# One RWKV-7 and FoX encoder block on one core: the correlation operand of a head pair written for both heads by one VectorE instruction each, the second head's half copied to its tile by ScalarE

## The chip, the core and the metric

The kernel runs on one core of one Trainium2 chip. The metric is the device time of one execution in microseconds. A core has five engines with a queue each, which work side by side and wait for one another by semaphores: TensorE (PE in the profile, its weight loads PEld), VectorE (DVE), ScalarE (ACT), GpSimd (POOL) and SyncE (SP, here only the issuing of transfers). Each queue is worked off in order.

## What is computed

One layer on 512 frames of 1024 channels: a half-step SwiGLU block, then two token mixers side by side on one input projection, then a second half-step block and a norm. The part that matters is the RWKV-7 mixer with 8 heads of 64:

```
kk = k * k_k;  kk = kk / max(sqrt(sum(kk * kk)), 1e-12)      # per head
k  = k * (1 + (a - 1) * k_a)
step: sa    = state . a_t                                     # a_t = -kk, b_t = kk * a
      state = state * w_t + sa b_t^T + v_t k_t^T
      y_t   = state . r_t
```

The kernel runs this recurrence over chunks of 32 frames. Within a chunk it needs the products of the "write" rows (kk·a and k, divided by the running decay) with the "read" rows (-kk and r, times the running decay), masked to the lower triangle, and the inverse of a triangular matrix made of them.

## The kernel before

All weights come as float32, and most products are done as three matmuls of a high and a low part (`mm3`, lines 170 to 172). For each block of 128 columns of the input projection there is a load (L155, SyncE), a high part by ScalarE (`whi`, L162), a low part by VectorE (`wlo`, L163), 24 matmuls of 128 by 512 into a PSUM bank (`pk`, `pgt` for a gate, `pv` later for FoX's v), and then one VectorE instruction that scales the result by the norm (`u`, L1223, or `gs`, L1253).

The 8 heads are 4 pairs; a pair lies on 128 partitions, one head in each half. `step(p)`, called for p = 0 to 3, prepares one pair. It runs the columns k, r and v of the pair and one gate. In between:

- k and r are shifted by a frame (ScalarE L1099, then VectorE L1100). ScalarE makes kk and its square, the square is split (`khi`, `klo`, L192 and L193) and summed over each head by two matmuls with a block matrix (`pn`, L1302 and L1303). ScalarE makes the inverse root `krn` in three steps (L1305, L1307, L1308), VectorE multiplies it in (L1309).
- VectorE scans the decays (L1289), ScalarE makes their two exponentials Pi and Pp (L1294, L1295).
- The write operand `BK[p]` holds k (L1297) and kk·a (L1312) for both heads on 128 partitions. The read operand is `G[p][q]`, one tile per head q of [128, 16 chunks, 2, 32]; head q's own half of the partitions takes -kk·Pp (L1315) and r·Pp (L1319).
- TensorE multiplies the two for each chunk and head (`gp`, L1329: 32 matmuls, each in two passes). The result goes, masked by VectorE (L1333, four instructions a pair), to the other half of `G[p][q]`, so that each tile holds operand and products. GpSimd stores the products to memory (Ld, L1341) for the inversion.
- r·k·r_k is summed over each head by two more matmuls (`rk` L1346, `rhi` and `rlo`, L1351 and L1352) for the bonus `bon`, which SyncE stores (L1356).

After the four pairs Ld is read back and VectorE inverts the triangular matrices (L1375, L1377), with weight splits in between. From then on the order of VectorE, ScalarE and TensorE is written out by hand. In `step` it is not: the order in which the instructions of the stage stand in each queue is set by the scheduler from the program's dependencies and its own estimate of times, except where a line ties one instruction behind another (`issue_after`). Thus an edit in `step` can move other instructions too.

Of the kernel before, what the change touches and what calls it, by code (L numbers as in the profile page):

```python
# [13 lines left out]
ALU = mybir.AluOpType  # L14
# [12 lines left out]
C = 32  # L27
# [50 lines left out]
def kernel(  # L78
# [24 lines left out]
    dve, act, pe = [Queued(e, False) for e in (nc.vector, nc.scalar, nc.tensor)]  # L103
# [14 lines left out]
    def bank(name, pool_=None):  # L118
        pool_ = pool_ or pm
        return pool_.tile([P, T], F32, tag="b", name=name)  # L120
# [70 lines left out]
    def split(dst_hi, dst_lo, src, hi_eng="act"):  # L191
        cast = act.copy(dst_hi, src) if hi_eng == "act" else dve.tensor_copy(dst_hi, src)  # L192
        return cast, dve.tensor_tensor(dst_lo, src, dst_hi.bitcast(F32), op=ALU.subtract)  # L193
# [7 lines left out]
    def on(do, *a):  # L201
        return lambda: do(*a)
# [95 lines left out]
    def pc(i):  # L298
        return par[:, i:i + 1]
# [345 lines left out]
    class Wide:  # L645
# [240 lines left out]
        def column(s, ps):  # L886
            s.rc = s.small[4]
            for i in range(2):
                pe.transpose(ps[:, i * P:(i + 1) * P], s.nrm.rstd[:, i * P:(i + 1) * P], ident[:])
            for i in range(2):  # L890
                dve.tensor_copy(s.rc[:, i:i + 1], ps[:, i * P:i * P + 1])
# [145 lines left out]
    op = o1.enter_context(tc.tile_pool(name="o1", bufs=1, side="right"))  # L1037
# [37 lines left out]
    with ExitStack() as mx:  # L1075
# [3 lines left out]
        G = [[sp.tile([P, NC, 2, C], F32, name=f"G{p}{q}", tag=f"G{p}{q}") for q in range(2)] for p in range(NP)]  # L1079
# [126 lines left out]
        ch = lambda t: t[:].rearrange("p (c t) -> p c t", t=C)  # L1206
        alt = {"Pi": Tall[:, 0:T], "kk": Tall[:, T:2 * T], "Pp": Tall[:, 2 * T:2 * T + NC * (C + 1)]}

        def prep(name, p, n=T):
            if p % 2 == 0:  # L1210
                return alt[name]
            t = t2.tile([P, n], F32, name=name, tag=name)
            return t[:]

        def work(name, dt=F32):
            late = name in ("kka", "rk", "bon")
            return t2.tile([P, T], dt, name=name, tag="sb" if late else "sa", bufs=3 if late else 5)
# [40 lines left out]
        def plain_gate(m):  # L1258
            gate = Gate(m)
            gate.go()  # L1260
            gate.out()
            return gate.mms
# [3 lines left out]
        def half(q):  # L1266
            return slice(q * 64, (q + 1) * 64)

        def step(p):
            if p % 3 == 0:  # L1270
                k, r = spare[2], spare[3]
            else:
                k, r = [t2.tile([P, T], F32, name=f"{n}{p}")[:] for n in "kr"]
            v = vs[p]
            cz, a = za[p]
            BK = BKs[p]
            if p:
                column(DA, p, k, 4)
            kk = prep("kk", p)
            act.activation(kk[:], k[:], AF.Copy, scale=pc(PAR_KK + p))  # L1280
            sq = work("ksq")
            act.activation(sq[:], kk[:], AF.Square)
            hi, lo = work("khi", F32R), work("klo", F32R)
            split(hi[:], lo[:], sq[:])
            t = work("kt")
            act.activation(t[:], a[:], AF.Identity, bias=nka[:, p:p + 1], scale=pc(PAR_KA + p))
            dve.scalar_tensor_tensor(k[:], t[:], 1.0, k[:], op0=ALU.add, op1=ALU.mult)
            with tc.issue_after(after[-1].ins) if after else ExitStack():
                dve.tensor_tensor_scan(cz[:], cmask[:], cz[:], initial=0.0, op0=ALU.mult, op1=ALU.add)  # L1289
            Pp = prep("Pp", p, NC * (C + 1)).rearrange("p (c t) -> p c t", t=C + 1)  # L1290
            pool.memset(Pp[:, :, 0:1], 1.0)
            Pi = prep("Pi", p)
            with tc.issue_after(logs.ins):
                act.activation(Pi[:], cz[:], AF.Exp, scale=DEC)  # L1294
                act.activation(Pp[:, :, 1:C + 1], ch(cz), AF.Exp, scale=-DEC)  # L1295
            pool.tensor_copy(PC[:, p, :], Pp[:, :, C])
            after.append(dve.tensor_tensor(BK[:, :, 1, :], ch(k), ch(Pi), op=ALU.mult))  # L1297

            mms = column(0, p, r, 0) if p else spread
            ps = bank("pn", pf)  # L1300
            with tc.issue_after(mms[2].ins):
                pe.matmul(ps[:], bonesr[:], hi[:], start=True, stop=False)  # L1302
                pe.matmul(ps[:], bonesr[:], lo[:], start=False, stop=True)  # L1303
            rn = work("krn")
            act.activation(rn[:], ps[:], AF.Relu, bias=tiny[:, 1:2])  # L1305
            with tc.issue_after(logs.ins):
                act.activation(rn[:], rn[:], AF.Ln, bias=tiny[:, 0:1])  # L1307
            act.activation(rn[:], rn[:], AF.Exp, scale=-0.5)  # L1308
            dve.tensor_tensor(kk[:], kk[:], rn[:], op=ALU.mult)  # L1309
            ka = work("kka")  # L1310
            dve.tensor_tensor(ka[:], kk[:], a[:], op=ALU.mult)
            dve.tensor_tensor(BK[:, :, 0, :], ch(ka), ch(Pi), op=ALU.mult)  # L1312
            for q in range(2):
                s = slice(q * 64, (q + 1) * 64)
                dve.scalar_tensor_tensor(G[p][q][s, :, 0, :], ch(kk)[s], -1.0, Pp[s, :, 0:C],  # L1315
                                         op0=ALU.mult, op1=ALU.mult)
            for q in range(2):
                s = slice(q * 64, (q + 1) * 64)
                dve.tensor_tensor(G[p][q][s, :, 1, :], ch(r)[s], Pp[s, :, 1:C + 1], op=ALU.mult)  # L1319
            column(2 * DA, p, v, 8)  # L1320
            mms = plain_gate(p)


            gps = [pr.tile([P, NC // 2, 2, C], F32, tag="b", name="gp") for _ in range(2)]
            with tc.issue_after(mms[5].ins):
                for c in range(NC):
                    for q in range(2):
                        o = half((q + c + 1) % 2)
                        gm = pe.matmul(gps[q][o, c // 2], BK[half(q), c], G[p][q][half(q), c], start=True, stop=True)  # L1329
            for q in range(2):  # L1330
                for odd in range(2):
                    o = half((q + odd + 1) % 2)
                    dve.tensor_tensor(  # L1333
                        G[p][q][half(1 - q), odd::2].rearrange("p c a t -> p c (a t)"),
                        gps[q][o].rearrange("p c a t -> p c (a t)"),
                        gmask[o].rearrange("p a t -> p (a t)").unsqueeze(1).broadcast_to([64, NC // 2, 2 * C]),
                        op=ALU.mult)
            for q in range(2):
                r0 = (1 - q) * 64
                un = (q * NP + p) * NC  # L1340
                nc.gpsimd.dma_start(Ld[un:un + NC].rearrange("c s t -> s c t"), G[p][q][r0:r0 + C, :, 0, :])  # L1341
                pool.memset(G[p][q][r0:r0 + C, :, 0, :], 0.0)


            rk = work("rk")
            dve.scalar_tensor_tensor(rk[:], r[:], pc(PAR_RK + p), k[:], op0=ALU.mult, op1=ALU.mult)  # L1346
            ps = bank("pn", pr)
            hi, lo = work("rhi", F32R), work("rlo", F32R)
            split(hi[:], lo[:], rk[:])
            with tc.issue_after(gm.ins):  # L1350
                pe.matmul(ps[:], bonesr[:], hi[:], start=True, stop=False)  # L1351
                pe.matmul(ps[:], bonesr[:], lo[:], start=False, stop=True)  # L1352
            bon = work("bon")
            dve.tensor_tensor(bon[:], ps[:], v[:], op=ALU.mult)
            act.activation(bon[:], bon[:], AF.Identity, bias=pc(PAR_LB + p))
            nc.sync.dma_start(bsave[p], bon[:])  # L1356

        for p in range(NP):
            step(p)
# [21 lines left out]
        for i in range(2):  # L1381
            for q in range(2):
                o = i * 64 + q * C
# [61 lines left out]
        for kg, (wh, wl) in enumerate(vw):  # L1445
            for b in range(NB):
                bs = slice(b * P, (b + 1) * P)
                for k in range(2):
                    kk = kg * 2 + k
                    mm3(vps[b][:], mix.hi[kk][:, bs], mix.lo[kk][:, bs], wh[:, k, :], wl[:, k, :],  # L1450
                        kk == 0, kk == KD - 1)
        for b in range(NB):
            o = vtp.tile([P, T], F32, name=f"vt{b}", tag=f"vt{b}")
# [39 lines left out]
        for q in range(2):  # L1493
            o = (1 - q) * 64
# [11 lines left out]
        for q in range(2):  # L1506
            o = (1 - q) * 64
# [9 lines left out]
        for q in range(2):  # L1517
            pool.memset(Rs[0][half(q), :, q, :], 0.0)
            for i in range(RN):
                o = (1 - q) * 64  # L1520
# [6 lines left out]
        op = plan.op  # L1527
        summed, gone = [op("SP", 0.0, None, later=us, frees=frees) for us, frees in ((3.0, ()), (3.5, ["w"]))]
        o = op("ACT", 0.69, b1.log, summed, rank=SCAN, takes=["t"], frees=["pf"])
        o = op("ACT", 0.63, b1.root, o, rank=SCAN)  # L1530
# [197 lines left out]
        for m in range(NP + 3, 2 * KD):  # L1728
            g = Held()
            w, o = columns("pgt", COL_GA + m * P)  # L1730
# [11 lines left out]
            o = op("DVE", 0.61, result, o, rank=NEXT, takes=["gs"], frees=["pm"])  # L1742
            if m + 1 < 2 * KD:
                o = op("ACT", 0.55 if tanhs else 1.84, opened, o, *roots, rank=ROWS)
# [150 lines left out]
        o = []  # L1895
        for p in range(NP):
            o = op("ACT", 0.63, on(part_y, p), *outs[p], *sees, *o, rank=FILL)
            o = [op("DVE", 0.69, on(part_l, p), o, rank=FILL)]
# [292 lines left out]
```

## Time and profile before

| | |
|---|---|
| runs | 1089.47 us median of 3 (1088.84 to 1091.12) |
| profiled execution | 1088.9 us, span 1087.0 us |
| granted TensorE clock, mean | 0.998 |
| `step`, the four pairs | about 367 to 460 us of the span |
| read operand writes, L1315 and L1319 | 16 of 64 by 512, about 0.68 us each |
| mask multiplies, L1333 | 16 of 64 by 512, 0.69 us each |

The page has the busy time of each engine, the span in 40 slices, the chain of work that ended last and the costliest groups of instructions. A row of the timeline has the start, the duration, the engine, the line, the operation, what is written and read, and in brackets the idle time of the engine before it with what ended it. Matmuls overlap: a row of 0.39 us is followed by the next after 0.23 us. A row of the chain has start, duration and what ran.

### The profile page before, as it was taken

What the parts mean: (1) busy time and instruction counts of PE and PEld (TensorE: products, weight loads), DVE (VectorE), ACT (ScalarE), POOL (GpSimd) and SP (SyncE); (2) the same over time, 40 slices, a digit from 0 to 9 for tenths busy, and PEclk for the clock granted to TensorE, in tenths of its full rate; (3) what the DMA queues carried; (4) which work ended last, traced back from release to release, by engine and by line L of the source; (5) the groups of instructions that cost most, each with busy time, mean ns of one, the idle gap of its engine ahead of it and who ended that gap; (6) DMA issues with size and microseconds to landing.
All of it is one profiled execution on the core that took longest, in us unless ns stands there. A gap on an engine that the chain in (4) does not pass through costs nothing.

```text
span 1087.0 us, 16960 instructions
## 1 busy us (share of the span) xinstructions
PE 1076.6 (99%) x6442; PEld 880.3 (81%) x6442; DVE 839.1 (77%) x1163; ACT 669.2 (62%) x1051; POOL 210.7 (19%) x255
## 2 busy tenths in 40 slices
PE   9999999999999999999999999999999999999997
PEld 7888888888887887788777777888888888888886
DVE  7997676789865689878777867867597766699874
ACT  6765556575655755435889776524576555576654
POOL 1221220134203202311000030122311212114210
PEclk9999999999999999999999999999999999999999
DMA  7989888879936334354223244635967978869972
GB/s 222 253 174 235 203 174 205 183 148 189 232 118 179 104 104 117 110 145 125 60 60 94 81 130 145 198 117 191 255 153 177 202 205 185 191 151 202 236 188 78
DMA packets 139726, 177.13 MB, mean 163 GB/s; under 512 B 9726, under 2 KB 75838, under 8 KB 139646
## 3 DMA queue, kind: packets, MB, share of 16 engines
q0 software_dynamic: 33328, 70.40, 34.0%
q1 hardware_dynamic: 105582, 104.21, 31.3%
q10 hardware_dynamic: 736, 1.45, 0.3%
q8 instruction: 51, 0.84, 0.3%
q14 instruction: 29, 0.24, 0.1%
HBM read 163.51 MB, written 12.52 MB: 162 GB/s over the span
## 4 chain that ended last, share of the span: by engine, by line
PE 93%; DVE 5%; ACT 1%; issue 1%; DVEq 0%; ACTq 0%
PE P L98 39%; PE P L172 5%; PE P L171 5%; PE P L170 5%; PE pgt L98 5%; PE spot L98 3%; PE lp L98 3%; PE pq L98 3%; PE ppj L98 2%; PE pb L98 2%; PE pa L98 2%; PE pw L171 1%; PE pw L170 1%; PE pw L172 1%; PE f L98 1%; DVE wlo L163 1%
## 5 line engine op out<-in xcount | busy, mean ns | idle before, releaser
L98 PE MATMUL P<-sraw,q 128*128 128x512 f32 x344 | 91.3, 389 | 0.0
L162 ACT CAST whi<-raw 128x1024 fp32r<-128x1024 f32 (+2 forms) x42 | 40.4, 962 | 59.0 <-issue 19.3
L98 PEld LDWEIGHTS P<-sraw,q 128*128 128x128 f32 x344 | 64.6, 188 | 13.4
L98 PE MATMUL P<-swhi,q 128*128 128x512 f32 x224 | 71.5, 390 | 0.0
L98 PE MATMUL P<-sraw,wxh 128*128 128x512 f32 x200 | 68.4, 394 | 0.0
L163 DVE TENSOR_TENSOR wlo<-raw,whi 128x1024 fp32r<-128x1024 f32 (+2 forms) x43 | 48.3, 1123 | 12.5 <-ACT whi L162 11.3
L98 PE MATMUL P<-swhi,wxh 128*128 128x512 f32 x144 | 57.0, 396 | 0.0
L98 PE MATMUL P<-swhi,wxl 128*128 128x512 f32 x144 | 56.2, 390 | 0.0
L98 PE MATMUL P<-swlo,wxh 128*128 128x512 f32 x144 | 56.1, 390 | 0.0
L688 POOL DMA_DIRECT2D cb<-in_ffn_w_dram x20 | 24.1, 1204 | 150.0 <-DVE cd L98 85.1
L98 PE MATMUL P<-sraw,wxl 128*128 128x512 f32 x136 | 53.0, 390 | 0.0
L688 POOL DMA_DIRECT2D cd<-in_ffn_w_dram x24 | 29.5, 1228 | 103.0 <-DVE swlo L98 38.6
L98 PEld LDWEIGHTS P<-swhi,q 128*128 128x128 f32 x224 | 42.1, 188 | 8.7
L98 ACT COPY RD<-spot 32x128 f32<-32x128 f32 (+2 forms) x128 | 39.8, 311 | 13.8 <-PE spot L98 11.4
L98 PE MATMUL P<-swlo,q 128*128 128x512 f32 x112 | 43.6, 389 | 0.0
L98 PEld LDWEIGHTS P<-sraw,wxh 128*128 128x128 f32 x200 | 37.2, 188 | 7.3
L98 ACT CAST sraw<-cd 128x1024 fp32r<-128x1024 f32 x30 | 31.5, 1051 | 15.0 <-PE P L98 11.5
L98 DVE TENSOR_TENSOR swlo<-ca,swhi 128x1024 fp32r<-128x1024 f32 x24 | 29.2, 1222 | 14.0 <-ACT swhi L98 14.0
L98 DVE TENSOR_TENSOR swlo<-cc,swhi 128x1024 fp32r<-128x1024 f32 x20 | 24.5, 1224 | 19.0 <-ACT swhi L98 18.7
L98 DVE TENSOR_TENSOR u<-P,u 128x512 f32<-128x512 f32 x52 | 34.1, 684 | 5.8 <-ACT u L98 5.8
L170 PE MATMUL pk<-xh,whi 128*128 128x512 f32 x96 | 38.0, 396 | 0.4 <-DVE u L1223 0.4
L547 POOL DMA_DIRECT2D ca<-in_ffn_w_dram x16 | 19.3, 1205 | 96.4 <-DVE swlo L98 66.4
(621 smaller groups left out, 3431.5 us busy)
## 6 DMA issues: line engine op xcount, KB each, us to landing
raw<-in_w_in_dram SPq DMA_DIRECT2D x40, 512.0 KB
cc<-in_ffn_w_dram SPq DMA_DIRECT2D x36, 512.0 KB
cb<-in_ffn_w_dram POOLq DMA_DIRECT2D x36, 512.0 KB, 5.9
cb<-in_ffn_w_dram SPq DMA_DIRECT2D x32, 512.0 KB
cd<-in_ffn_w_dram POOLq DMA_DIRECT2D x32, 512.0 KB, 7.7
ca<-in_ffn_w_dram POOLq DMA_DIRECT2D x32, 512.0 KB, 7.1
ca<-in_ffn_w_dram SPq DMA_DIRECT2D x20, 512.0 KB
cd<-in_ffn_w_dram SPq DMA_DIRECT2D x18, 512.0 KB
```

The lines of the kernel that those rows point to most:

```text
L98: q.last = do(*a, **kw)
L162: (hi_eng or act).copy(hi[:], raw[:])
L163: (eng or dve).tensor_tensor(lo[:], raw[:], hi[:].bitcast(F32), op=ALU.subtract)
L170: pe.matmul(ps, whi, xhi, start=first, stop=False, skip_group_check=onto)
L171: pe.matmul(ps, whi, xlo, start=False, stop=False, skip_group_check=onto)
L172: return pe.matmul(ps, wlo, xhi, start=False, stop=last, skip_group_check=onto)
L547: nc.gpsimd.dma_start(s.sum[g], src, accum_op=ALU.add)
L688: nc.gpsimd.dma_start(to, s.block(b, n, h), accum_op=ALU.add)
```

## The change

The r and kk parts of the read operand are written for both heads at once, into the first head's tile, by one VectorE instruction each over 128 partitions. ScalarE then copies the second head's half of that tile into the same place of the second head's tile. TensorE's correlation reads both heads' operand from the first tile. The lines behind it have moved up by four: L1329 is L1325, the masks L1333 are L1329, L1351 is L1347 and so on.

```diff
-            for q in range(2):
-                s = slice(q * 64, (q + 1) * 64)
-                dve.scalar_tensor_tensor(G[p][q][s, :, 0, :], ch(kk)[s], -1.0, Pp[s, :, 0:C],
-                                         op0=ALU.mult, op1=ALU.mult)
-            for q in range(2):
-                s = slice(q * 64, (q + 1) * 64)
-                dve.tensor_tensor(G[p][q][s, :, 1, :], ch(r)[s], Pp[s, :, 1:C + 1], op=ALU.mult)
+            dve.scalar_tensor_tensor(G[p][0][:, :, 0, :], ch(kk), -1.0, Pp[:, :, 0:C], op0=ALU.mult, op1=ALU.mult)
+            dve.tensor_tensor(G[p][0][:, :, 1, :], ch(r), Pp[:, :, 1:C + 1], op=ALU.mult)
+            act.copy(G[p][1][half(1)], G[p][0][half(1)])
             column(2 * DA, p, v, 8)
             mms = plain_gate(p)
...
-                        gm = pe.matmul(gps[q][o, c // 2], BK[half(q), c], G[p][q][half(q), c], start=True, stop=True)
+                        gm = pe.matmul(gps[q][o, c // 2], BK[half(q), c], G[p][0][half(q), c], start=True, stop=True)
```

Since the scheduler sets the order, all three engines' queues change in this stage. On TensorE, the rows around the correlation of pair 1 (`G_2540` and `G_2541` are the pair's two tiles, `pn` the head sums, `pk` a column, `pgt` gate 2), before:

```order
L1329 MATMUL gp<-G_2541,BK_2547 64x64
L1351 MATMUL pn<-rhi,bonesr 128x512
L1352 MATMUL pn<-rlo,bonesr 128x512
L1302 MATMUL pn<-khi,bonesr 128x512
L1303 MATMUL pn<-klo,bonesr 128x512
L172 MATMUL pgt<-xh_2584,wlo 128x512
```

and after:

```order
L170 MATMUL pk<-xh_2584,whi 128x512
L171 MATMUL pk<-xl_2585,whi 128x512
L1325 MATMUL gp<-G_2540,BK_2547 64x64 x32
L1347 MATMUL pn<-rhi,bonesr 128x512
L1348 MATMUL pn<-rlo,bonesr 128x512
L172 MATMUL pk<-xh_2584,wlo 128x512
```

The block stood two matmuls into gate 2; it now stands two matmuls into the v column of pair 2, which is 24 matmuls earlier, and the sums of pair 2's squares (`khi`, `klo`) have left it: they come 17 matmuls further on, and 14 apart.

Again on TensorE, the rows from the correlation of pair 2 (`G_2542` and `G_2543`) to the first sum of pair 3's squares, before:

```order
L1329 MATMUL gp<-G_2543,BK_2548 64x64
L1351 MATMUL pn<-rhi,bonesr 128x512
L1352 MATMUL pn<-rlo,bonesr 128x512
L170 MATMUL pk<-xh_2584,whi 128x512
L171 MATMUL pk<-xl_2585,whi 128x512
L172 MATMUL pk<-xh_2584,wlo 128x512
L1302 MATMUL pn<-khi,bonesr 128x512
```

and after:

```order
L1325 MATMUL gp<-G_2542,BK_2548 64x64 x32
L1347 MATMUL pn<-rhi,bonesr 128x512
L1348 MATMUL pn<-rlo,bonesr 128x512
L171 MATMUL pk<-xl_2445,whi 128x512
L172 MATMUL pk<-xh_2444,wlo 128x512
L170 MATMUL pk<-xh_2478,whi 128x512
L171 MATMUL pk<-xl_2479,whi 128x512
L172 MATMUL pk<-xh_2478,wlo 128x512
L170 MATMUL pk<-xh_2478,whi 128x512
L171 MATMUL pk<-xl_2479,whi 128x512
L172 MATMUL pk<-xh_2478,wlo 128x512
L1302 MATMUL pn<-khi,bonesr 128x512
```

The correlation stood at the end of pair 3's r column and now stands eight matmuls before that end; the first sum of pair 3's squares stood three matmuls into the v column and now stands just behind the r column's last matmul.

On VectorE, the rows of pair 2 from the scaled kk (L1309) to the last write of BK; the weight split among them (L163) is that of pair 3's r column. Before:

```order
L1309 TENSOR_TENSOR Tall<-Tall,krn 128x512
L1253 TENSOR_TENSOR gs<-pgt,rstd 128x512
L163 TENSOR_TENSOR wlo<-raw,whi 128x1024
L1311 TENSOR_TENSOR kka<-Tall,BK_2549 128x512
L1315 SCALAR_TENSOR_TENSOR G_2542<-Tall 64x16x32
L1315 SCALAR_TENSOR_TENSOR G_2543<-Tall 64x16x32
L1346 SCALAR_TENSOR_TENSOR rk<-r_3192,par,k_3191 128x512
L1312 TENSOR_TENSOR BK_2548<-kka,Tall 128x16x32
```

and after:

```order
L1309 TENSOR_TENSOR Tall<-Tall,krn 128x512
L1253 TENSOR_TENSOR gs<-pgt,rstd 128x512
L1311 TENSOR_TENSOR kka<-Tall,BK_2549 128x512
L1313 SCALAR_TENSOR_TENSOR G_2542<-Tall 128x16x32
L1342 SCALAR_TENSOR_TENSOR rk<-r_3190,par,k_3189 128x512
L163 TENSOR_TENSOR wlo<-raw,whi 128x1024
L1312 TENSOR_TENSOR BK_2548<-kka,Tall 128x16x32
```

The split of the r column's weights has moved behind the read operand and r·k. On ScalarE each copy (L1315) stands just ahead of the high part of r·k (`rhi`, L192), behind a weight cast.

## The prediction

> **What bounds the kernel now.** I read the page first, then the table by stretches, then TensorE's waits, then the chain of waits and the timeline at the few places where TensorE stands still.
>
> ```profile
> PE 1076.6 (99%) x6442; PEld 880.3 (81%) x6442; DVE 839.1 (77%) x1163; ACT 669.2 (62%) x1051; POOL 210.7 (19%) x255
> ...
> 410.00:420.00 10.00, 9.93 (x102) 7.80 (x101) 9.94 (x16) 7.07 (x11) 0.65 (x2) 1.00 0.53 137
> 420.00:430.00 10.00, 9.99 (x43) 7.63 (x42) 9.87 (x14) 5.34 (x8) 2.88 (x5) 1.00 0.34 94
> 430.00:440.00 10.00, 8.24 (x94) 6.39 (x94) 8.19 (x12) 4.88 (x9) 2.18 (x3) 1.00 0.45 133
> ```
>
> TensorE is busy 1076.6 us of 1087.0, so all that any change off TensorE can win is 10.4 us, and most of that is the first and the last moments of the program. The three stretches of 10 us (columns: TensorE, weight load, VectorE, ScalarE, GpSimd, granted clock, DMA) lie in the stage that the change edits. Here VectorE is full (9.94 and 9.87 of 10) while ScalarE is half empty, and here TensorE loses 1.76 us in one stretch. The granted clock is 1.00 throughout. So the question is not how much VectorE work goes, but how much of TensorE's standing still in this stage goes with it.
>
> ```profile
> PE pn L1302 <- ACT khi L192: 1.4, 1, 1.4
> ...
> 434.18 1.13 DVE wlo L163
> ...
> 435.83 0.75 DVE spare L1100
> ...
> 436.61 0.73 ACT kk L1280
> ...
> 437.90 0.15 ACT whi L162
> 438.05 0.78 issue
> 438.83 0.62 ACT khi L192
> ...
> 439.50 0.50 PE pn L1302
> ```
>
> The longest wait is pair 3's head sum (L1302), and the chain behind it runs through VectorE's queue: the shift of k (L1100) stands behind the weight split (L163). The timeline gives the exact size of each halt, as start to start minus the plain pitch of 0.23 us (417.64 to 417.87).
>
> ```profile
> 397.08 0.39 PE L170 MATMUL pk<-xh,whi 128*128 128x512 f32 x1
> ...
> 417.64 0.39 PE L1352 MATMUL pn<-rlo,bonesr 128*128 128x512 f32 x1
> 417.87 0.40 PE L1302 MATMUL pn<-khi,bonesr 128*128 128x512 f32 x1
> 418.34 0.50 PE L1303 MATMUL pn<-klo,bonesr 128*128 128x512 f32 x1
> 418.67 0.39 PE L172 MATMUL pgt<-xh,wlo 128*128 128x512 f32 x1
> ...
> 428.92 0.39 PE L172 MATMUL pk<-xh,wlo 128*128 128x512 f32 x1
> 429.31 0.47 PE L170 MATMUL pk<-xh,whi 128*128 128x512 f32 x1
> 429.62 0.40 PE L171 MATMUL pk<-xl,whi 128*128 128x512 f32 x1
> 430.35 0.50 PE L172 MATMUL pk<-xh,wlo 128*128 128x512 f32 x1 [0.34 <-DVE wlo L163]
> 430.68 0.39 PE L170 MATMUL pk<-xh,whi 128*128 128x512 f32 x1
> ...
> 437.68 0.40 PE L172 MATMUL pk<-xh,wlo 128*128 128x512 f32 x1
> 439.50 0.50 PE L1302 MATMUL pn<-khi,bonesr 128*128 128x512 f32 x1 [1.43 <-ACT khi L192]
> 439.84 0.40 PE L170 MATMUL pk<-xh,whi 128*128 128x512 f32 x1
> ```
>
> Three halts: (a) at 418, pair 2's klo is late: 0.24, and 0.10 until the pitch is regained, 0.34 us. (b) At 429 to 431 the low weights of pair 3's r column come late: 0.16 + 0.08 + 0.50 + 0.10 = 0.84 us. (c) At 439.50: 1.59 + 0.11 = 1.70 us. Together 2.88 us. A fourth, 0.2 us, is the rlo of pair 3 near 456:
>
> ```profile
>   DVE rlo L193: 0.2, 1
> ```
>
> Nothing after 460 shows TensorE waiting, so what is won here should arrive at the end whole.
>
> **The change, part by part.** VectorE first: what two halves and one whole cost in this very queue.
>
> ```profile
> 391.30 1.38 DVE L1319 TENSOR_TENSOR G<-r,Pp 64x512 f32<-64x512 f32 x2
> 392.71 0.69 DVE L1311 TENSOR_TENSOR kka<-Tall,G 128x512 f32<-128x512 f32 x1
> 393.32 1.37 DVE L1315 SCALAR_TENSOR_TENSOR G<-Tall 64x512 f32<-64x512 f32 x2
> 394.73 0.75 DVE L1346 SCALAR_TENSOR_TENSOR rk<-spare,par 128x512 f32<-128x512 f32 x1
> ...
> 395.99 1.21 DVE L163 TENSOR_TENSOR wlo<-raw,whi 128x1024 fp32r<-128x1024 f32 x1
> 397.13 0.68 DVE L1312 TENSOR_TENSOR BK<-kka,Tall 128x512 f32<-128x512 f32 x1
> 397.73 0.68 DVE L193 TENSOR_TENSOR rlo<-rk,rhi 128x512 fp32r<-128x512 f32 x1
> ```
>
> Two halves hold the queue 1.41 us (391.30 to 392.71, 393.32 to 394.73). One instruction over 128 partitions, written into the same strided layout (BK, L1312), holds it 0.60 (397.13 to 397.73). Each of the eight replaced couples saves 0.81 us, 1.62 a pair and 6.5 in all. The other bound is by the busy times alone, 1.38 - 0.68 = 0.70 a couple, 5.6 in all; I take 0.81, since the queue is full and its pitch is what counts.
>
> The Trainium skill ("VectorE: DVE Perf Modes", section "Two Vector instructions with no wait between them") says that an instruction whose output starts in another group of 32 partitions than the one before it starts only when all before it are finished. By that rule the halves cannot overlap their neighbours and the whole can, which gives the 0.81; without it the saving would be the 0.70, and the stage's sum the lower of the two. The trace agrees with it here: the halves stand 0.70 apart, the wholes 0.60.
>
> ScalarE gets four copies of 64 by 1024. No row has this shape. The nearest are the casts of 128 by 1024 and a 64 by 512 copy:
>
> ```profile
> L162 ACT CAST whi<-raw 128x1024 fp32r<-128x1024 f32 x25 | 26.1, 1046 | 29.6 <-PE pv L172 9.2 <-PE pgt L171 8.6 <-PE pq L171 7.8
> ...
> L1153 ACT COPY low<-pl 64x512 f32<-64x512 f32 x1 | 0.6, 582 | 0.0
> ```
>
> So between 0.58 and 1.05 us; I take 1.0, by the row with as many elements in a line. That is 4 us on an engine with 3 to 5 us free in every 10. The copy waits for the kk write, and stands just ahead of rhi, which waits for r·k, the next VectorE instruction (0.66 later). So rhi comes 0.3 to 0.4 later after its input than before; rlo is hidden by the weight split that VectorE does in between (1.14). The correlation (gp) reads only the first head's tile now and does not wait for the copy; the mask multiply does, but comes 2 us or more after it.
>
> The order of the queues moves far more than the edit. I walked VectorE, ScalarE and TensorE in their new orders from the row at 388.89, each instruction starting at the later of its queue's pitch and its input, with pitches from the rows above: 0.60 for 128 by 512, 0.66 for L1100 and r·k, 1.14 for a weight split or a scan, 2.85 for the four mask multiplies, 0.94 for a ScalarE cast of 1024, 0.23 a matmul, 1.09 a gp block. What TensorE meets:
>
> - Pair 1's gp, 24 matmuls (5.5 us) earlier: TensorE arrives at 410.8, BK is done at 409.0; r·k's low half at 410.7, wanted at 411.9. No wait, margins 1.8 and 1.1.
> - Pair 2's klo now has 14 matmuls between khi's sum and its own: done 418.4, wanted 419.7. **Halt (a) goes: 0.34.**
> - Pair 3's k weights: VectorE reaches the split only after r2 shifted (414.25), four masks (to 417.75), klo, G, bon, k, BK (five times 0.60 to 420.75), the scan (421.9) and u (422.5): done 423.65, wanted 423.8. No wait, margin 0.15.
> - Pair 3's r weights: ScalarE shifts v when u is there, then makes krn in three steps; VectorE waits for that.
>
> ```profile
> 419.04 0.71 ACT L1099 ACTIVATE V<-u,omu 128x512 f32<-128x512 f32 x1
> 419.66 0.67 ACT L1305 ACTIVATE krn<-pn,small 128x512 f32<-128x512 f32 x1
> 420.36 0.72 ACT L1307 ACTIVATE krn<-krn,small 128x512 f32<-128x512 f32 x1
> 421.11 0.64 ACT L1308 ACTIVATE krn<-krn 128x512 f32<-128x512 f32 x1
> ```
>
> These four take 2.7 us from start to end (419.04 to 421.75). With two exponentials ahead (to 423.1) krn is there at 425.7. VectorE idles until then, about 1 us, and does kk, gs, ka, the whole G write and r·k (to 428.8) before the split: done 430.0, wanted 429.3. **Halt (b) stays, 0.75 instead of 0.84: 0.1 won.**
> - Pair 3's head sum: after the split BK, rlo and u (431.7), ScalarE's scaled copy (432.4), the shift (433.5), kk, square, khi without a weight cast in between (1.9): done 435.3. The sum now stands behind the last eight matmuls of the r column. From 397.08 there are 144 matmuls (32.8), three gp blocks with their entries (3.6), ten head sums (2.7) and 0.75 of halt: TensorE arrives at 436.8. **Halt (c) goes: 1.70.**
> - Pair 3's gp is 21 matmuls earlier, at 449.0; BK is done at 447.5, rlo at 449.2 and wanted at 450.1. **The 0.2 goes.**
>
> Sum: 0.34 + 0.1 + 1.70 + 0.2 = 2.3 us. Behind the stage comes the triangular inversion on VectorE, which waits for pair 3's masked products on their way through memory:
>
> ```profile
> 467.19 0.19 DVE L1375 TENSOR_TENSOR prod<-TT,Ls 128x31 f32<-128x31 f32 x1 [1.50 <-DMA Ls<-Ld]
> ```
>
> In the walk pair 3's masks come some 5 us earlier, so the inversion starts near 462, while TensorE is only 2.3 us ahead; that lead also covers the store of TT, which ScalarE now issues ahead of one weight cast instead of behind it. Without the lead that cast, and TensorE behind it, would wait for the end of the inversion. On SyncE two stores of bon each move ahead of one weight load. Both loads wait for a weight split that comes later than the store's input (423.65 against 420.4, 441.9 against 440.3), so the queue costs nothing; without that cover the load would wait for bon. GpSimd's stores of Ld only come earlier, with the masks.
>
> The profiled execution took 1088.9 us, its span and 1.9 around it; the median shown is 1089.47, 0.57 above. With 2.3 off, the profiled time would be 1086.6 and the median **1087.2 us**, minus 0.21%.
>
> **Rivals.**
>
> 1. Halt (b) goes too. VectorE would have to be 0.6 us earlier at the r weights. For it: a full us of that queue is idling for krn, which hangs on one ScalarE instruction. Against it: ScalarE has five instructions between. It gives 0.75 more, 3.05 in all: 1086.4.
> 2. The thin margins eat the gain: it becomes "about the same". The walk has 0.15 at the k weights, and every change of engine in it may cost 0.1 more than I gave it. With VectorE 1 us later than walked, TensorE halts 0.85 at the k weights, and at the r weights 0.15 more than walked, 1.0 in all. For it: VectorE is the full engine, 9.9 of 10. Against it: before, the same hand-overs were in the rows that I used. It gives 1088.2.
> 3. Slower, by one mechanism: TensorE takes its queue in order, and gp of pair 1 with its two sums is put 5.5 us earlier in it. Whatever VectorE is late there beyond the margin of 1.1 us stops the whole queue, us for us. From 3.4 us of lateness the gain is gone, from 5.6 the kernel is slower by 0.2%; at 5 us it is 1.6 slower, 1091.1. That would also be the picture of a whole write that is no cheaper than two halves: three couples lie before this point, 2.4 us. The L1312 row speaks against it.
>
> **How the numbers follow.** The forecast, 1.6 to 2.8 us won, has 0.47; rival 1 has 0.20; rival 2, with less than 1.6 won, 0.24; rival 3 has 0.09. About 0.2%, 2.18 us, is what a measurement of this kernel can tell from no change; the forecast stands on that edge, half of it (0.24) beyond. Faster by over 0.2% is then 0.24 + 0.20 = 0.44; within 0.2% the other 0.23 of the forecast, 0.24 and 0.02 of rival 3, 0.49; slower by over 0.2% the rest of rival 3, 0.07. The range takes in rival 1 with the runs' spread below (0.6, median to lowest) and rival 2 down to no gain: 1085.7 to 1089.7.
>
> **What would show it.** In the profile after: L1314 and L1313 four times each at 0.68 us, over 128 partitions; L1315 four times near 1.0. TensorE's waits no longer list L1302 behind khi; the list has the r weights (L172 behind wlo) with a few tenths. The stretch 430 to 440 shows TensorE above 9.2. VectorE's busy time falls by about 5.5. The inversion (L1371) starts near 462. Wrong would be a TensorE wait at L1325 or L1347, a wait of the masks (L1329) for L1315, or a halt after 460 that takes the gain back.

## The result, and the profile after

| | before | after |
|---|---|---|
| median of 22 runs each, side by side | 1089.47 us (1088.70 to 1091.12) | 1087.99 us (1087.37 to 1088.80) |
| ratio after to before, 95% interval | | 0.9987, 0.9981 to 0.9993 |
| profiled execution, span | 1088.9, 1087.0 us | 1088.02, 1086.2 us |
| mean granted clock | 0.998 | 0.998 |

The kernel is 1.48 us faster, 0.14%. The forecast was 1087.2 us, a gain of 2.3; the measured gain lies below the 1.6 to 2.8 us that the forecast stood for, and the time is nearest to the second rival (1088.2).

First the page's busy times, then TensorE's waits, then the two stretches from 420 to 440 (length, TensorE, weight load, VectorE, ScalarE, GpSimd, granted clock, DMA share, GB/s).

```profile
PE 1076.7 (99%) x6442; PEld 880.5 (81%) x6442; DVE 834.0 (77%) x1155; ACT 673.5 (62%) x1055; POOL 210.8 (19%) x255
```

```profile
PE warm L307 <- DVE onesr L132: 1.1, 1, 1.1
PE pk L172 <- DVE wlo L163: 1.0, 2, 0.7
...
```

```profile
420.00:430.00 10.00, 9.66 (x42) 7.45 (x41) 8.57 (x13) 6.72 (x10) 1.93 (x4) 1.00 0.31 95
430.00:440.00 10.00, 9.33 (x100) 7.17 (x99) 7.79 (x12) 6.66 (x9) 2.33 (x2) 1.00 0.41 124
```

VectorE has lost 5.1 us of work and ScalarE has gained 4.3. The wait of 1.4 us behind khi (L1302) is gone, and the stretch 430 to 440 has TensorE at 9.33 where it was 8.24. But L172 behind wlo now stands twice in the list, and the stretch 420 to 430, where TensorE was full (9.99), has lost a third of a microsecond. The timeline of TensorE shows the two places:

```profile
423.65 0.39 PE L172 MATMUL pgt<-xh,wlo 128*128 128x512 f32 x1
423.97 0.47 PE L170 MATMUL pk<-xh,whi 128*128 128x512 f32 x1
424.27 0.40 PE L171 MATMUL pk<-xl,whi 128*128 128x512 f32 x1
425.01 0.50 PE L172 MATMUL pk<-xh,wlo 128*128 128x512 f32 x1 [0.34 <-DVE wlo L163]
425.34 0.39 PE L170 MATMUL pk<-xh,whi 128*128 128x512 f32 x1
...
430.36 0.39 PE L171 MATMUL pk<-xl,whi 128*128 128x512 f32 x1
431.41 0.50 PE L172 MATMUL pk<-xh,wlo 128*128 128x512 f32 x1 [0.67 <-DVE wlo L163]
431.75 0.40 PE L170 MATMUL pk<-xh,whi 128*128 128x512 f32 x1
432.00 0.40 PE L171 MATMUL pk<-xl,whi 128*128 128x512 f32 x1
```

Counted as in the prediction (start to start less 0.23 us), pair 3's k weights cost 0.09 + 0.07 + 0.51 + 0.10 = **0.77 us** where nothing was expected, and pair 3's r weights 0.82 + 0.11 + 0.02 = **0.95 us** where 0.75 was. The other halts, (a), (c) and the 0.2 near 456, are gone. The account is then 0.34 + 1.70 + 0.2 won, 0.77 lost at the k weights and 0.95 - 0.84 = 0.11 lost at the r weights: 1.36 us, against 1.48 between the medians.

The two profiled executions themselves differ by 0.88 us only. The reason lies ahead of the stage: from 21 us of the span on, TensorE, VectorE and ScalarE all stand 0.45 us later in the profile after. At 464 us TensorE is 0.70 ahead of before, and at its last matmul 0.89, so 1.34 us are won between the stage's start and the end. Of these 1.15 are won in the stage, 0.2 less than the account says; that rest is spread over many rows, and its cause is not known. The other 0.18 are won behind the stage, at 503 us: before, TensorE met a late operand there (`pq`, L98, the second of two head sums), and now it does not. The profiles of the experiments have such offsets too, from 0.11 early to 0.65 late against before. Where times of two profiles are compared below, the text says what the offset makes of them.

What VectorE does on the way to these two weight splits (start, duration, line, what is written and read, idle time before it):

```profile
413.97 1.23 DVE L163 TENSOR_TENSOR wlo<-raw,whi 128x1024 fp32r<-128x1024 f32 x1 [1.13 <-ACT whi L162]
415.12 0.75 DVE L1100 SCALAR_TENSOR_TENSOR r<-u,par,r 128x511 f32<-128x511 f32 x1
415.90 2.83 DVE L1329 TENSOR_TENSOR G<-gp,gmask 64x512 f32<-64x512 f32 x4
418.76 0.69 DVE L193 TENSOR_TENSOR klo<-ksq,khi 128x512 fp32r<-128x512 f32 x1
419.37 0.69 DVE L1314 TENSOR_TENSOR G<-r,Tall 128x512 f32<-128x512 f32 x1
420.09 0.69 DVE L1350 TENSOR_TENSOR bon<-pn,V 128x512 f32<-128x512 f32 x1
420.70 0.68 DVE L1287 SCALAR_TENSOR_TENSOR k<-kt,k 128x512 f32<-128x512 f32 x1
421.41 0.69 DVE L1297 TENSOR_TENSOR BK<-k,Tall 128x512 f32<-128x512 f32 x1
422.02 1.22 DVE L1289 TENSOR_TENSOR_SCAN spare<-cmask,spare 128x512 f32<-128x512 f32 x1
423.16 0.66 DVE L1223 TENSOR_TENSOR u<-pk,rstd 128x512 f32<-128x512 f32 x1
423.74 1.21 DVE L163 TENSOR_TENSOR wlo<-raw,whi 128x1024 fp32r<-128x1024 f32 x1
...
427.07 0.69 DVE L1309 TENSOR_TENSOR Tall<-Tall,krn 128x512 f32<-128x512 f32 x1 [1.25 <-ACT krn L1308]
...
428.88 0.68 DVE L1313 SCALAR_TENSOR_TENSOR G<-Tall 128x512 f32<-128x512 f32 x1
429.48 0.74 DVE L1342 SCALAR_TENSOR_TENSOR rk<-r,par,k 128x512 f32<-128x512 f32 x1
430.14 1.22 DVE L163 TENSOR_TENSOR wlo<-raw,whi 128x1024 fp32r<-128x1024 f32 x1
```

The reader is to see three things. The whole read-operand write (L1313, L1314) is cheap, as costed: 0.60 us until the next row at 428.88. VectorE is not a full queue here any more: it idles 1.13 us for a weight cast and 1.25 us for krn. And both late splits (423.74 and 430.14) start without idle time in front: their input was there, and other VectorE work stood ahead of them.

### The profile page after: what moved, and what is told of

Same layout as the page of the kernel before. It is cut to its first block, busy times and chain, and to the rows that moved or that the text cites. A ratio compares the mean times of both kernels' runs of the same rounds, so it can differ in the third digit from the quotient of the medians.

```text
span 1086.2 us, 16961 instructions
## 1 busy us (share of the span) xinstructions
PE 1076.7 (99%) x6442; PEld 880.5 (81%) x6442; DVE 834.0 (77%) x1155; ACT 673.5 (62%) x1055; POOL 210.8 (19%) x255
## 4 chain that ended last, share of the span: by engine, by line
PE 97%; DVE 1%; ACT 1%; issue 0%; DMA 0%; DVEq 0%; ACTq 0%
PE P L98 39%; PE P L172 6%; PE P L171 6%; PE P L170 5%; PE pgt L98 5%; PE spot L98 3%; PE lp L98 3%; PE pq L98 3%; PE ppj L98 2%; PE pk L170 2%; PE pk L172 2%; PE pk L171 2%; PE pb L98 2%; PE pa L98 2%; PE pw L171 1%; PE pw L170 1%
## 5 line engine op out<-in xcount | busy, mean ns | idle before, releaser
L98 PE MATMUL P<-sraw,q 128*128 128x512 f32 x344 | 91.3, 389 | 0.0
L98 PEld LDWEIGHTS P<-sraw,q 128*128 128x128 f32 x344 | 64.6, 188 | 13.4
L98 PE MATMUL P<-swhi,q 128*128 128x512 f32 x224 | 71.4, 390 | 0.0
L98 PE MATMUL P<-sraw,wxh 128*128 128x512 f32 x200 | 68.4, 394 | 0.0
L98 PE MATMUL P<-swhi,wxh 128*128 128x512 f32 x144 | 56.9, 395 | 0.0
L98 PE MATMUL P<-swhi,wxl 128*128 128x512 f32 x144 | 56.1, 390 | 0.0
L98 PE MATMUL P<-swlo,wxh 128*128 128x512 f32 x144 | 56.1, 389 | 0.0
L163 DVE TENSOR_TENSOR wlo<-raw,whi 128x1024 fp32r<-128x1024 f32 (+2 forms) x43 | 48.5, 1127 | 9.5 <-ACT whi L162 8.3
L98 PE MATMUL P<-sraw,wxl 128*128 128x512 f32 x136 | 53.0, 390 | 0.0
L98 PEld LDWEIGHTS P<-swhi,q 128*128 128x128 f32 x224 | 42.0, 188 | 8.7
L98 ACT COPY RD<-spot 32x128 f32<-32x128 f32 (+2 forms) x128 | 39.8, 311 | 13.9 <-PE spot L98 11.6
L98 PE MATMUL P<-swlo,q 128*128 128x512 f32 x112 | 43.6, 389 | 0.0
L98 PEld LDWEIGHTS P<-sraw,wxh 128*128 128x128 f32 x200 | 37.2, 188 | 7.3
L98 ACT CAST sraw<-cd 128x1024 fp32r<-128x1024 f32 x30 | 31.5, 1050 | 15.5 <-PE P L98 11.5
L98 DVE TENSOR_TENSOR swlo<-ca,swhi 128x1024 fp32r<-128x1024 f32 x24 | 29.2, 1222 | 13.9 <-ACT swhi L98 13.9
L98 DVE TENSOR_TENSOR swlo<-cc,swhi 128x1024 fp32r<-128x1024 f32 x20 | 24.5, 1224 | 18.5 <-ACT swhi L98 18.2
L98 DVE TENSOR_TENSOR u<-P,u 128x512 f32<-128x512 f32 x52 | 34.1, 684 | 5.8 <-ACT u L98 5.7
L172 PE MATMUL pk<-xh,wlo 128*128 128x512 f32 x96 | 37.5, 392 | 1.0 <-DVE wlo L163 1.0
```

The lines of the kernel that those rows point to most:

```text
L98: q.last = do(*a, **kw)
L163: (eng or dve).tensor_tensor(lo[:], raw[:], hi[:].bitcast(F32), op=ALU.subtract)
L172: return pe.matmul(ps, wlo, xhi, start=False, stop=last, skip_group_check=onto)
```

## Experiments

All kernels below compute the whole function. Each was timed in five rounds beside the kernel before on the same chip, whose median there was 1088.96 us for the halves on VectorE, the copy on GpSimd, the order alone and the scan behind the split, 1089.12 for kk in halves, the change once more, the exponentials behind krn and both ties, and 1089.19 for the last.

**Is it the freed VectorE queue, or the correlation reading one tile?** The change also lets the correlation wait for fewer writes. Here the copy by ScalarE is replaced by two half writes on VectorE, while the whole writes and TensorE's reading stay as changed:

```diff
-            act.copy(G[p][1][half(1)], G[p][0][half(1)])
+            s = half(1)
+            dve.scalar_tensor_tensor(G[p][1][s, :, 0, :], ch(kk)[s], -1.0, Pp[s, :, 0:C], op0=ALU.mult, op1=ALU.mult)
+            dve.tensor_tensor(G[p][1][s, :, 1, :], ch(r)[s], Pp[s, :, 1:C + 1], op=ALU.mult)
```

> Whole writes into the first head's tile as in the change, but the second head's half is written once more by VectorE (two 64 by 512 instructions a pair) instead of copied by ScalarE; TensorE still reads both heads from the first tile. VectorE thus pays 0.60 + 0.70 a couple, about what it paid before (1.41). Theory Q (the gain is VectorE's queue being relieved): 1089.0 to 1089.9, TensorE's wait at L1302 behind khi is back with 1.0 to 1.8 us. Theory R (the gain is TensorE reading one tile instead of two): 1088.0, no wait at L1302.

Measured 1089.48 us, ratio 1.0005 (0.9996 to 1.0014): the whole gain is gone. TensorE's order is that of before again, row for row, and so are its long waits:

```profile
PE pn L1302 <- ACT khi L192: 1.4, 1, 1.4
...
PE pk L172 <- DVE wlo L163: 0.3, 1, 0.3
```

The gain needs the time saved on VectorE. Reading one tile alone is worth nothing.

**Does the engine that copies matter?** The same copy on GpSimd:

```diff
-            act.copy(G[p][1][half(1)], G[p][0][half(1)])
+            pool.tensor_copy(G[p][1][half(1)], G[p][0][half(1)])
```

> The change with the copy on GpSimd instead of ScalarE; the rows of VectorE and TensorE stand in the same order as in the change. Theory Q says the copy on ScalarE is covered: 1088.0 within 0.4, the two halts at the k and r weights of pair 3 (0.77 and 0.95 us) stay within 0.3. Theory S (what was missing from 2.3 us went into ScalarE's queue behind the copies): 1087.2, both halts smaller by about 0.4. If GpSimd's copy takes more than 4 us the masks wait for it and the time rises above 1088.5.

Measured 1089.26 us, ratio 1.0002 (0.9993 to 1.0010); neither number was met. ScalarE is relieved, yet the gain is gone. The timeline shows where; GpSimd's copy, the r weights' split on VectorE and the matmul that waits for it, each from its engine's rows:

```profile
429.86 1.43 POOL L1315 COPY G<-G 64x1024 f32<-64x1024 f32 x1 [0.46 <-DVE G L1313]
```

```profile
429.65 0.74 DVE L1342 SCALAR_TENSOR_TENSOR rk<-r,par,k 128x512 f32<-128x512 f32 x1
430.31 2.06 DVE L163 TENSOR_TENSOR wlo<-raw,whi 128x1024 fp32r<-128x1024 f32 x1
```

```profile
432.42 0.50 PE L172 MATMUL pk<-xh,wlo 128*128 128x512 f32 x1 [1.51 <-DVE wlo L163]
```

The split takes 2.06 us instead of 1.21 while the copy runs, and TensorE pays for it: its halt at the r weights grows from 0.95 to 1.78 us. Pair 3's bonus sums come late too (0.32 us more; BK, ahead of their operand on VectorE, took 1.27 us beside its copy), and the halt at the k weights has 0.24 more, 0.17 of it put down to the exponential Pi, for a reason that stays open. Together that is 1.39 us, about all that the change had won. So the copying engine matters, though by a cost that none of the theories held.

**Is the new order of TensorE a gain by itself?** The kernel before, its halves untouched, with ties that put the correlations of pairs 0 to 2 about as early in TensorE's queue as the change does (`gms` collects the last matmul of each correlation; the matmuls of the named column from that place on are tied behind it):

```diff
+        gms = []
+        BEHIND = {(DA, 2): (0, 0), (2 * DA, 2): (1, 0), (0, 3): (2, 5)}
...
+            g, k0 = BEHIND.get((c0, p), (0, KD))
+            mms = mix.cols(ps[:], *w, P, ks=range(k0), end=k0 == KD) if k0 else []
+            if k0 < KD:
+                mms += mix.cols(ps[:], *w, P, [gms[g]] * (KD - k0), ks=range(k0, KD), begin=k0 == 0)
...
+            gms.append(gm)
```

> The kernel before, with its two halves of operand writes, but three ties that put the k column of pair 2 behind gp of pair 0, the v column of pair 2 behind gp of pair 1, and the last three parts of the r column of pair 3 behind gp of pair 2, so that gp stands about as early in TensorE's queue as in the change. Theory O (the gain is the new order on TensorE, whatever VectorE does): 1088.3 or less. Theory Q: gp and its sums now stand ahead of what VectorE has ready; TensorE waits at gp or at the sums of rhi and rlo for 1 us or more at least twice, and the time is 1091 or more.

Measured 1099.79 us (four runs), ratio 1.0103 (1.0089 to 1.0116): 10.8 us slower. TensorE's waits, and its rows at the correlation of pair 1 (L1336 in this kernel):

```profile
PE gp L1336 <- DVE BK L1319: 5.8, 2, 5.2
PE pk L172 <- DVE wlo L163: 2.6, 1, 2.6
...
PE pq L98 <- DVE l L98: 1.1, 1, 1.1
```

```profile
416.24 1.99 PE L1336 MATMUL gp<-G,BK 64*64 64x64 f32 x64 [5.24 <-DVE BK L1319]
418.15 0.79 PE L1359 MATMUL pn<-rhi,bonesr 128*128 128x512 f32 x1
```

The early correlation pays only when VectorE is early too. With the halves in VectorE's queue it is a trap: this is the third rival's mechanism, at its place.

**How much of VectorE's saving is needed?** The change with kk's write in two halves again (into the first tile), so that each pair saves 0.81 us and not 1.62:

```diff
-            dve.scalar_tensor_tensor(G[p][0][:, :, 0, :], ch(kk), -1.0, Pp[:, :, 0:C], op0=ALU.mult, op1=ALU.mult)
+            for s in (half(0), half(1)):
+                dve.scalar_tensor_tensor(G[p][0][s, :, 0, :], ch(kk)[s], -1.0, Pp[s, :, 0:C], op0=ALU.mult, op1=ALU.mult)
```

> The change with half of its relief: r is written whole, kk in two halves (both into the first head's tile), ScalarE copies as in the change. VectorE pays 0.8 us a pair more than in the change. Theory Q: the halts at pair 3's weights are longer than the change's 1.7 together, by 0.5 to 1.6, and the time lies between the change and the kernel before or above; with the order that the scheduler gives it, gp is as early as in the change, so it may end slower than the kernel before. Theory R (not VectorE's queue): the time of the change, the same halts.

Measured 1089.39 us, ratio 1.0003 (0.9994 to 1.0012). Half the saving gives none of the gain. The halves hold the queue 1.42 us (r·k follows at 429.48) where the whole held 0.60, and both stand right ahead of the r weights' split. That split begins at 430.14 by the profile's time; with the offset between the two profiles (0.53) taken off, it is 0.53 later than under the change, though kk's scaling (L1309, at 426.25) is 0.29 earlier:

```profile
428.06 1.38 DVE L1314 SCALAR_TENSOR_TENSOR G<-Tall 64x512 f32<-64x512 f32 x2
```

```profile
PE pk L172 <- DVE wlo L163: 1.7, 2, 1.5
...
PE pn L1349 <- DVE rlo L193: 0.5, 1, 0.5
...
PE gp L1326 <- DVE BK L1312: 0.2, 1, 0.2
```

By TensorE's timeline the halt at the k weights is 0.27 smaller than under the change, that at the r weights 0.82 larger, and two halts in pair 3's correlation and its sums come to 0.25 and 0.62: 1.42 us worse in all, which is also the distance of the medians (1089.39 to 1087.97 below). At this place the 0.82 us more on VectorE in front of the split are 0.82 us more of TensorE's halt.

**The change once more,** beside the kernels that follow:

> The change itself once more, beside the kernel before on this chip, as the measure for the runs sent with it. Both halts (0.77 at the k weights, 0.95 at the r weights of pair 3) are there again, none at L1302; 1.0 to 1.8 us below the kernel before.

Measured 1087.97 us, ratio 0.9988 (0.9979 to 0.9997), with the same waits of TensorE and the two longest gaps within 0.01 us of those above.

**Are the two late splits what is left?** Three kernels move what stands ahead of them. First the scan of pair 3 (L1289), 1.14 us just ahead of the k weights' split, is tied behind that split (`splits` collects the splits of weights):

```diff
-            with tc.issue_after(after[-1].ins) if after else ExitStack():
+            with tc.issue_after((splits if p == 3 else after)[-1].ins) if after else ExitStack():
```

> The change with one tie: the decay scan of pair 3 (1.14 us on VectorE) stands behind the weight split of pair 3's k column instead of ahead of it. Theory Q with the shortfall in VectorE's lateness at the weight splits: the halt of 0.77 us at the k weights (L172 behind wlo near 425) goes or falls below 0.2, the halt at the r weights (0.95) stays or grows by up to 0.5, since krn comes later; 1087.0 to 1087.8. If the halts only trade places, 1088.0.

Measured 1089.27 us, ratio 1.0003 (0.9994 to 1.0012). The halt at the k weights is gone, and the one at the r weights is 2.14 us:

```profile
431.73 0.50 PE L172 MATMUL pk<-xh,wlo 128*128 128x512 f32 x1 [1.87 <-DVE wlo L163]
```

The scan feeds the two exponentials of pair 3 (L1294, L1295), which stand ahead of krn's last two steps on ScalarE; krn comes later, and VectorE idles for it 1.85 us instead of 1.25. The halts trade places and grow by 0.42 us together. The profiled execution, 1088.17 us, lies only 0.15 above the change's; nine of the other ten were 1.0 to 1.5 us above it, and what these lost no trace shows.

Second, only the exponentials move: they are tied behind the last step of pair 2's krn (`roots` collects those), so that krn no longer stands behind them.

```diff
-            with tc.issue_after(logs.ins):
+            with tc.issue_after(roots[-1].ins if p == 3 else logs.ins):
                 act.activation(Pi[:], cz[:], AF.Exp, scale=DEC)
                 act.activation(Pp[:, :, 1:C + 1], ch(cz), AF.Exp, scale=-DEC)
...
-            act.activation(rn[:], rn[:], AF.Exp, scale=-0.5)
+            roots.append(act.activation(rn[:], rn[:], AF.Exp, scale=-0.5))
```

> The change with one tie: ScalarE makes pair 3's decay exponentials behind pair 2's inverse root (krn) instead of ahead of it. Theory K (the halt at the r weights hangs on krn, for which VectorE idles 1.25 us): krn 1.0 to 1.3 us earlier, VectorE's idle time before L1309 below 0.3, the r weights early enough, the halt of 0.95 goes or falls below 0.3; the halt at the k weights stays near 0.77; 0.5 to 1.0 us below the change. Theory V (VectorE is simply full there): VectorE fills the idle time with other work and the halt stays above 0.7; the time of the change.

Measured 1086.97 us, ratio 0.9979 (0.9971 to 0.9988), 1.0 below the change, inside the 0.5 to 1.0 of the theory that the r weights' halt hangs on krn. The halt at the k weights is as under the change, that at the r weights is gone; pair 2's sums now cost 0.27, so the rows show some 0.7 of the 1.0. But the way is not the expected one: VectorE still idles 1.00 us for krn. Rows of VectorE, then of TensorE:

```profile
426.45 0.69 DVE L1309 TENSOR_TENSOR Tall<-Tall,krn 128x512 f32<-128x512 f32 x1 [1.00 <-ACT krn L1308]
427.17 0.69 DVE L1311 TENSOR_TENSOR kka<-Tall,BK 128x512 f32<-128x512 f32 x1
...
429.67 0.67 DVE L1312 TENSOR_TENSOR BK<-kka,Tall 128x512 f32<-128x512 f32 x1
430.26 1.21 DVE L163 TENSOR_TENSOR wlo<-raw,whi 128x1024 fp32r<-128x1024 f32 x1
```

```profile
430.54 1.16 PE L1325 MATMUL gp<-G,BK 64*64 64x64 f32 x64
...
432.47 0.39 PE L172 MATMUL pk<-xh,wlo 128*128 128x512 f32 x1
```

L1309 stands at 426.45, 427.07 under the change; with the offset (0.13) taken off, krn is there 0.49 earlier, not 1.0 to 1.3, since ScalarE now idles 1.37 us for u ahead of it. The split is not earlier: it starts at 430.26 (430.14 under the change), with BK now ahead of it. BK being earlier, the scheduler has put pair 2's correlation and its two sums ahead of the matmul that waited for the split, so TensorE has 1.9 us of other rows, the 0.27 of waiting among them, at the place where it stood still.

Third, both ties:

> The change with both ties: pair 3's scan behind the split of its k weights, and pair 3's decay exponentials behind pair 2's krn. Theory K: both halts fall below 0.3, unless TensorE now meets gp of pair 2 before BK; 1.0 to 1.7 us below the change, 2.3 to 3.2 below the kernel before. Theory V: the halts trade places again, as with the scan's tie alone; the time of the change.

Measured 1085.84 us (five runs, 1085.33 to 1086.14), ratio 0.9968 (0.9956 to 0.9981): 2.1 us below the change and 3.3 below the kernel before, the fastest of all. TensorE's waits, and VectorE's split of the k weights, behind which the scan now stands:

```profile
PE warm L307 <- DVE onesr L132: 1.1, 1, 1.1
PE pk L170 <- DVE u L1223: 0.4, 1, 0.4
```

```profile
422.10 1.22 DVE L163 TENSOR_TENSOR wlo<-raw,whi 128x1024 fp32r<-128x1024 f32 x1
```

Neither line belongs to a weight split, and from 380 to 460 us TensorE's rows have no gap. With the offset (0.50) taken off, the k weights' split starts 1.14 us earlier than under the change, which is the scan's time, and VectorE no longer idles for krn. The tie that brings nothing alone (scan behind the split) wins here, because the other has taken the exponentials out of krn's way. The two halts that are gone come to 1.72 us; TensorE's rows gain 1.84 on the change, the medians 2.1, and the rest no row shows.

**Do the ties need the change?** The same two ties on the kernel before:

> The two ties of the run before (pair 3's scan behind the split of its k weights, pair 3's two decay exponentials behind pair 2's inverse root) on the kernel before the change. TensorE's order is then that of before, row for row; of VectorE's only the scan moves, from behind BK to the place behind the split, and of ScalarE's the two exponentials move ahead of a weight cast. Theory U (the ties spend room in VectorE's queue that only the change makes): VectorE has as much to do as before ahead of pair 3's head sum, so the halt of 1.70 us behind khi stays within 0.5 of itself, and the time is within 0.6 us of before. Theory T (the ties are a gain of their own, the change has no part in it): about 2.1 us below before, as they were below the change.

Measured 1088.92 us, ratio 0.9998 (0.9989 to 1.0007): no gain. TensorE's wait behind khi (L1302, 1.4 us) is in its list again. The ties only place the room that the change makes in VectorE's queue; without the room they do nothing.

## Why the prediction was right, and where it was off

- **Which halts go: right for three of four.** Halts (a) and (c) and the 0.2 went, 2.24 us. The halves on VectorE bring them back, the order alone loses 10.8 us, and with half the saving new halts take the whole gain: it takes the new order and VectorE's time together. Halt (b) was to stay with 0.1 won; it stayed with 0.11 lost. The first rival wanted the r weights' split 0.6 earlier; where the halt went in a later run, it went by TensorE's order with the split no earlier.
- **The term that was mis-sized is the margin of 0.15 us at pair 3's k weights** ("done 423.65, wanted 423.8. No wait"). It came out as a halt of 0.77. TensorE came to pair 1's correlation at 411.26 here, 0.46 later than the walk had it (410.8); that is the offset with which this profile starts, and the whole walk is shifted by it. VectorE was later still. The split before the shift of r waited 1.13 us for ScalarE's weight cast, which stood behind pair 2's kk:

```profile
412.28 0.72 ACT L1280 ACTIVATE Tall<-k,par 128x512 f32<-128x512 f32 x1 [1.88 <-DVE k L1100]
412.90 1.03 ACT L162 CAST whi<-raw 128x1024 fp32r<-128x1024 f32 x1
```

  It started at 413.97, walked 413.1 (the prediction's 414.25 is where the shift behind it starts, 1.14 later): 0.41 late beyond the 0.46. The masks start 0.78 behind the shift where 0.66 was given, 0.12 more; the profile before had this pair too, 0.76 apart (421.95 to 422.71), and the walk did not use it. From klo to the scan (418.76 to 422.02) are five steps, 3.26 us, where five times 0.60 was given, 0.26 more: bon starts 0.72 behind G, and BK 0.71 behind k, which it reads. Together 0.79; less the margin that is 0.64, and 0.10 to regain the pitch makes 0.74 of the 0.77. The 0.71 behind k looks like the price of reading what the instruction in front has just written: in the run with the exponentials behind krn, kka stands directly behind kk and starts 0.72 after it (426.45, 427.17), and under the change, with one instruction between, each step was 0.60 to 0.61. What bon waits for no run shows; in the run with kk in halves it starts 0.71 behind another neighbour, klo (418.56, 419.27).
- **So the second rival's mechanism came true, at its place and nearly at its size:** it had VectorE 1 us late, 0.85 at the k weights and 0.15 more at the r weights, 1.0 lost; measured 0.77 and 0.20 (0.95 for 0.75), 0.97. The argument held against it ("before, the same hand-overs were in the rows that I used") was the wrong one: most of the instructions follow one another in another order now, and a pitch belongs to a pair of neighbours at least, not to an instruction.
- **Durations: right.** The whole writes take 0.68 and hold the queue 0.60, as said; VectorE's busy time fell by 5.1 (5.5 said); the copies take 1.04 to 1.05 (1.0 said):

```profile
429.59 1.05 ACT L1315 COPY G<-G 64x1024 f32<-64x1024 f32 x1 [1.61 <-DVE G L1313]
```

  The halves in the run with kk in halves hold the queue 1.42 us again, so the 0.81 a couple, and with it the rule on held instructions (the Trainium skill, "VectorE: DVE Perf Modes", section "Two Vector instructions with no wait between them"), agrees with what was measured.
- **The waits that were denied did not come:** no wait at the correlation, none of the masks for the copy, none after 460. The inversion starts at 464.02, 3.2 us earlier than before (467.19; 3.6 with the offset taken off), not 5; VectorE idles 3.42 us there for the transfer that reads Ld back:

```profile
464.02 0.19 DVE L1371 TENSOR_TENSOR prod<-TT,Ls 128x31 f32<-128x31 f32 x1 [3.42 <-DMA Ls<-Ld]
```

  That cost TensorE nothing. The stretch 430 to 440 was said to pass 9.2 and stands at 9.33.
- **Two small slips.** "Nothing after 460 shows TensorE waiting" misses the late sum at 503, worth 0.18. The terms of TensorE's way to pair 3's head sum add up to 436.9, not 436.8; the operand was there in time, so nothing hangs on it.
- **The third rival was priced too low.** "Us for us" does not hold: in the run with the order alone the late correlation of 5.3 us cost TensorE 7.6, as the last section works out.

## What to carry to other kernels

Before times of two profiles are compared, the offset that they bring along from ahead of the changed stage is to be taken off; here it was 0.45 us, a third of the gain. Time taken off a full queue is worth the halts that end with it, and the halt that comes next is found by walking the new order to the next hand-over; where such a walk leaves a margin smaller than the error it has gathered (here 0.15 us after some ten steps, off by 0.8), that margin is to be counted as a halt. Pitches for the walk come from pairs of neighbours: whether an instruction reads what the one in front of it wrote, and what its releaser stands behind. Once the room is made, a look at what stands ready in front of the late instruction can be worth more than the change itself: two ties gave another 2.1 us here, and nothing without the room, and part of it by other work that filled the wait, not by an earlier split.

## What the runs showed of the hardware

- **VectorE and GpSimd held each other up.** GpSimd's copy of 64 by 1024 took 1.05 us at its fastest (pair 3's) and 1.43 beside VectorE's r·k; VectorE's weight split took 1.21 us elsewhere and 2.06 beside the copy. The split began at 430.31, the copy ended at 429.86 + 1.43 = 431.29, and the split ended 1.08 after that, about its own length. That is the picture of the split standing still until the copy was done. Beside the other three copies BK's write (L1312) took 0.92 to 1.27 us instead of 0.68 and ended 0.54 after the copy each time, while u (L1223), which reads one of its two inputs from PSUM, stayed at 0.68 beside the copies. The Trainium skill has it so ("SBUF — State Buffer", section "Who interferes with whom": a VectorE instruction with two inputs in SBUF contends with a GpSimd instruction that reads SBUF, and the one that is issued second is blocked for all of the first); the rows agree. ScalarE's copy of the same shape left the split at 1.22.
- **The long halts of TensorE cost more than themselves.** In the run with the order alone the granted clock was 0.50 from 414.5 us, still within the wait of 5.24 us, to 421.3, and 0.51 from 434.9, right behind the wait of 2.57 us, to 438.3. The stretch behind the wait of 5.24 us has a clock of 0.50:

```profile
415.00:420.00 5.00, 3.76 (x68) 3.32 (x69) 4.99 (x8) 3.21 (x5) 0.00 (x0) 0.50 0.32 87
```

  The correlation took 1.91 us instead of 1.09, and the matmuls after it followed one another every 0.43 instead of 0.23 until 421: 5.3 us of halt and 2.3 of slow clock. The wait of 2.57 us at the r weights did the same, 2.7 and 1.7. Together with 0.7 at pair 0's correlation and 1.1 at pq, less the 3.1 of halts that before has, that is 10.7 of the 10.8 us lost. Halts of up to 1.87 us of waiting, in all the other runs, left the clock at 1.00. The Trainium skill ("TensorE: Matmul & The Clock Gate", section "Why this matters for your kernels") names gaps of over about 3 us as those after which the clock falls; here one of 2.57 was enough.
